# ScalarE and VectorE take the recorded order, and branch D's sums and attention's pauses move

## The chip, the cores and the metric

The kernel runs on one core of a Trainium2 chip. The metric is the device time of one execution in microseconds. Five engines of the core work beside each other: TensorE (PE in the profile, its weight loads PEld) multiplies matrices, ScalarE (ACT) applies functions element by element and copies, VectorE (DVE) does arithmetic on one or two tiles, GpSimd (POOL) does little here, and SyncE (SP) starts most DMAs. Each engine works through its own list of instructions in order, and semaphores make one engine wait for another.

## The reference

Two layers of a hybrid encoder over x (256 tokens, 2048 channels, float32), then a final RMSNorm:

```python
h = rms_norm(x, norm_g)
proj = h @ w_in                       # 2048 x 15104: inputs of the branches A, B, C, D, and four merge gates
ya = a_bg * depthwise_conv(a_cg * a_x, conv_a_w) * silu(a_z)                  # A: 3 taps
yb = gqa_attention(rope(rms_norm(q)), rope(rms_norm(k)), v) * silu(b_z)       # B: 8 query heads, 2 kv heads
yc = rwkv7_bidir(h, c_r, c_k, c_v, ...) * silu(c_z)                           # C: a recurrence in both directions
yd = silu(layer_norm(depthwise_conv(d_val * sigmoid(d_gate), dw_w))) * silu(d_z)   # D: 31 taps
bp = einsum('bskc,kcd->bskd', stack([ya, yb, yc, yd]), w_branch)              # four products 512 x 2048
x = x + (sum over branches of sigmoid(gates) * bp) @ w_out                    # 2048 x 2048
```

## The kernel before

**The stream of weights.** The weights of a layer come as 306 chunks of 128 x 1024 float32 (512 KB), 612 in all. SP starts a DMA for each into one of 4 buffers `raw` (`load`). ScalarE copies a chunk, rounded, to `hi` (`fetch`, 3 buffers), VectorE computes `lo` = raw - hi (`low`, 2 buffers). TensorE multiplies with both, the operand being held as a rounded part and a rest too. For most tiles (`tile_b`, two chunks, PSUM tile `mg`, 3 buffers) a chunk is 8 matmuls 512 wide on `hi`, then 8 matmuls 256 wide on `lo`, called the lo pass here. For a branch's product (`tile_branch`, PSUM tile `mb`) a chunk is 24 matmuls 256 wide. When chunk n begins on TensorE, `chunk` records `lo` of chunk n + 1 and `hi` of chunk n + 2; the two buffers of `lo` let lo n + 1 begin only when the lo pass of chunk n - 1 is over. After a `tile_b`, `whole` and `evac` move its sum out: a ScalarE copy of one half of PSUM, then a VectorE add of the other half, both short but on the same two engines. In the rows below, chunk 0 is the first of the kernel.

**The side work.** Everything else runs beside the stream: the norm at the layer's start (`normalise`), the head norms and rotary positions of attention (`head_rstd`, `norm_rope`), attention (`branch_b`), the convolutions (`branch_a`, `conv_d`, `branch_d`), the preparation of the recurrence for two pairs of heads and two directions (`rwkv`: decay, norm of k, cumulative products; `chunks`, and `inverses`, a triangular solve whose substitution is 31 pairs of dependent VectorE operations on 64 partitions), and the recurrence. These are Python generators. `pump`, called after each pair of matmuls while the program is recorded, advances a generator by its next piece when a planner's clocks allow it. A generator yields a pause: a positive number counts from now, a negative one (`HP` -2.5, `PM` -1.5, `LN` -3.6) from the time at which the planner expects the piece's last result. The planner charges each instruction a fixed price. The planner's clocks decide what is recorded between which matmuls.

**Who keeps that order.** `run` records both layers under `manual_schedule(engines={PE})`: TensorE's list is the recorded order. The lists of ScalarE and VectorE are laid out by the framework's scheduler, which moves `hi`, `lo`, evacuation copies and a few more (recorded under `high_priority`) ahead of side work and takes other instructions as it expects them to become ready.

**Reciprocal square roots.** `rsqrt` is, on ScalarE, a table load, a logarithm, another table load and an exponential. The norms of heads (`parts`, then `exact`) split a square into two rounded tiles `part`, of which one pair of buffers exists, and sum it with two matmuls into a PSUM tile `sd`.

Of the kernel before, what the change touches and what calls it, by code (L numbers as in the profile page):

```python
# [18 lines left out]
P = 128  # L19
# [6 lines left out]
CH = 64  # L26
# [185 lines left out]
class Kern:  # L212
# [26 lines left out]
    def __init__(self, ctx, tc, io):  # L239
        self.tc, self.io = tc, io  # L240
        self.now = self.due = self.landed = 0.0
        self.clk = {"vector": 0.0, "scalar": 0.0}
        self.ring = [0.0] * 4
        self.rushing = False
        self.next = dict(self.clk)
        self.nc = Clocked(self)
        pool = lambda name, space=None: ctx.enter_context(
            tc.tile_pool(name=name, bufs=1, space=space) if space else tc.tile_pool(name=name, bufs=1))
        self.cst = pool("cst")
        self.wp = pool("wp")  # L250
        self.sp = pool("sp")
        self.ps = pool("ps", PSUM)
        self.dr = pool("dr", DRAM)
        self.n = 0
        self.side = []
        self.cur = None
        self.arena = Arena(self.cst.tile([P, self.ARENA], F32, name="arena"), self.ARENA)
# [388 lines left out]
        yield 1.1  # L646


    def parts(self, x):

        self.n += 1
        n = int(np.prod(x.shape[1:]))
        t = self.wp.tile([P, 2, 512], F32R, tag="part", bufs=self.PARTS, name=f"part_{self.n}")
        hi, lo = t[:, 0, :n], t[:, 1, :n]
        view = lambda a: a.rearrange("p (a t) -> p a t", a=x.shape[1]) if len(x.shape) > 2 else a
        self.nc.scalar.activation(view(hi), x, AF.Copy)
        self.nc.vector.tensor_tensor(view(lo), x, view(hi).bitcast(F32), ALU.subtract)
        return hi, lo

    def exact(self, ps, stationary, parts):  # L660

        hi, lo = parts
        self.nc.tensor.matmul(ps, stationary, hi, start=True, stop=False)
        return self.nc.tensor.matmul(ps, stationary, lo, start=False, stop=True)

    def head_rstd(self, x):

        nc = self.nc
        out = self.a1()
        nc.scalar.activation(out, x, AF.Square)  # L670
        parts = self.parts(out)
        yield self.HP
        ps = self.pside()[:, :S]
        self.rsqrt(ps, 1.0 / 64, self.e_rms, out, self.exact(ps, self.bdr, parts))
        yield 0
        return out

    def norm_rope(self, x, rs, g, dst):
# [2 lines left out]
        nc.vector.scalar_tensor_tensor(xn, x, g, rs, ALU.mult, ALU.mult)  # L681
        t = self.a1()
        nc.vector.tensor_tensor(t, xn, self.cos, ALU.mult)
        parts = self.parts(xn)
        yield self.HP
        ps = self.pside()
# [86 lines left out]
    def branch_d(self, acc, convs, dz):  # L773
        nc = self.nc
        for i in range(NT):
            while len(convs) <= i:
                yield 0.5
            yield from convs[i]
        while self.merged < 1:
            yield 0.5  # L780
        ys = self.ys[3] = self.operand()
        yield 0
        sq = self.a([P, 2, S])
        nc.vector.tensor_tensor(sq[:, 0:2], acc[:, 0:2], acc[:, 2:4], ALU.add)
        nc.vector.tensor_tensor(sq[:, 0], sq[:, 0], sq[:, 1], ALU.add)
        yield self.LN
        ps = self.pside()
        nc.tensor.matmul(ps[:, :S], self.ones, sq[:, 0], start=True, stop=True)
        for i in range(NT):
# [8 lines left out]

        rs = self.a1()
        self.rsqrt(ps[:, :S], 0.25 / W, self.e_ln, rs, made)  # L800
        yield 0
        for i in range(NT):
            while len(dz) <= i:
# [16 lines left out]
    def rwkv(self, rkv, tl, cz):  # L820
# [5 lines left out]
        for d in range(2):  # L826
# [8 lines left out]
            for p0 in range(0, NT, 2):  # L835
                pp = slice(p0, p0 + 2)
                v5 = lambda x: x.rearrange("p a (c t) -> p a c t", c=NCH)
                while self.cv < p0 + 1:
                    yield 0.5
                yield from self.room(3136)  # L840
                lbs = []
                for i in range(2):
                    lb = self.a([P, 2, P])
                    nc.gpsimd.dma_start(lb[:LORA], self.io["lorab"][l, d, :, :, (p0 + i) * P:(p0 + i + 1) * P])
                    lbs.append(lb)
                yield 0.3
# [22 lines left out]
                for i in range(2):  # L869
                    p, lb = p0 + i, lbs[i]  # L870
                    ps = self.pside()
                    for j in range(2):
                        nc.tensor.matmul(ps[:, j * S:(j + 1) * S], lb[:LORA, j], tl[j][d][:LORA], start=True, stop=True)
                    self.f(lb)
                    nc.scalar.activation(flip(sg[:, i]), ps[:, :S], AF.Tanh, scale=0.5, bias=self.w0h[:, d * NT + p:d * NT + p + 1])
                    nc.scalar.activation(flip(ai[:, i]), ps[:, S:], AF.Tanh, scale=0.5, bias=self.a0h[:, d * NT + p:d * NT + p + 1])
                    yield 0.8
                parts = self.parts(rs)
                yield self.PM
                ps = self.pside()  # L880
# [6 lines left out]
                for i in range(2):  # L887
                    nc.vector.tensor_tensor_scan(sg[:, i], self.scan, sg[:, i], 0.0, ALU.mult, ALU.add)

                pi = self.a([P, 2, NCH, CH + 1])  # L890
                nc.vector.memset(pi[:, :, :, 0:1], 1.0)
                nc.scalar.activation(pi[:, :, :, 1:], v5(sg), AF.Exp, scale=-DECAY)
                pv = sg
# [23 lines left out]
                self.f(ai)  # L917
                yield 1.0
                nc.scalar.activation(dend[:, pp], pi[:, :, :, CH], AF.Copy)
                self.f(pi)  # L920
                yield 0
                parts = self.parts(r2)
                yield self.PM
                ps = self.pside()
# [25 lines left out]
            if d == 1:  # L950
                self.f(*rkv)
            self.cur.want = 0

            yield 4.0
            yield from self.room(2304)
# [31 lines left out]
            for p in range(NT):  # L987
# [68 lines left out]

                sq = self.a([P, 2, S])
                nc.scalar.activation(sq, y2, AF.Square)
                parts = self.parts(sq)
                yield self.PM  # L1060
                ps = self.pside()
# [70 lines left out]
    def chunks(self, n, out, bd, al, vv, kb, gs, rd):  # L1132
# [39 lines left out]
            if h == 0:  # L1172
                yield 0.6
        out.append((ex, mk, w))
        yield self.PM


    def layer(self, l):
# [28 lines left out]
            self.bdr, self.permr = rounded[:, 0], rounded[:, 1]  # L1207
        self.ys = [None] * 4
        self.merged = 0
        got = {}  # L1210
        gens = [[] for _ in range(4)]
        acc = [None] * 8
# [171 lines left out]
    def run(self):  # L1384
# [3 lines left out]
        self.consts()  # L1388
        self.first_x()

        with self.tc.manual_schedule(engines={mybir.EngineType.PE}):
            for l in range(DEPTH):
                self.layer(l)

# [124 lines left out]
```

## Time and profile before

| | |
|---|---|
| time, median of 3 runs | 1965.2 us (1964.5 to 1965.85) |
| the profiled execution: time, span | 1966.2 us, 1964.2 us |
| mean granted TensorE clock of the span | 0.994 |
| PE, DVE, ACT busy | 1921.9, 1444.4, 1262.0 us |
| `lo`: 612 on DVE | 748.5 us busy, 1.223 us each |
| `hi`: 612 on ACT | 646.8 us busy, 1.057 us each |
| ACT table loads | 62, 1.283 us each |

Busy time is the union of an engine's instructions. The span runs from the first to the last instruction that the profile counts; the execution's own time is 2.0 us longer. The first matmul starts at 9.4 us, since it waits for x.

### The profile page before, as it was taken

How to read it: one execution, taken by the hardware profiler on the slowest of the kernel's cores; microseconds unless marked ns; L12 is line 12 of the kernel's file. 1: busy time of each engine (PE TensorE's matmuls, PEld its weight loads, DVE VectorE, ACT ScalarE, POOL GpSimd, SP SyncE). 2: the span in 40 equal slices, each digit the busy share in tenths (PEclk: the TensorE clock that was granted, in tenths of full speed). 3: DMA queues.
4: the chain of work that ended last, by engine and by line, in shares of the span. 5: the costliest groups of instructions: out<-in, count | busy, mean ns of one | idle time of the engine just before them, and what ended most of it. 6: DMA issues, size and time to landing. Idle time of an engine off the chain costs nothing.

```text
span 1964.2 us, 32326 instructions
## 1 busy us (share of the span) xinstructions
PE 1921.9 (98%) x12190; PEld 1704.5 (87%) x12190; DVE 1444.4 (74%) x2500; ACT 1262.0 (64%) x2292; POOL 72.3 (4%) x117
## 2 busy tenths in 40 slices
PE   8999999999999999999999999999999999999997
PEld 6888788899988998998888887888989889989886
DVE  7867979977787556666687778799677875565665
ACT  7777577667647776554467766776666477765544
POOL 2001010000001000000000011000001010000000
PEclk9999999999999999999999999999999999999998
DMA  7555454455556445566655555444555564455653
GB/s 254 178 176 173 159 159 131 152 176 178 178 179 189 150 152 176 195 210 207 206 193 178 176 172 162 136 151 150 172 176 185 169 180 152 151 185 195 207 194 129
DMA packets 97692, 343.17 MB, mean 175 GB/s; under 512 B 11808, under 2 KB 12192, under 8 KB 97536
## 3 DMA queue, kind: packets, MB, share of 16 engines
q1 hardware_dynamic: 93312, 331.48, 51.2%
q0 software_dynamic: 3648, 8.59, 1.8%
q8 instruction: 95, 1.56, 0.3%
q10 hardware_dynamic: 576, 1.05, 0.1%
q14 instruction: 61, 0.50, 0.1%
HBM read 332.48 MB, written 8.39 MB: 174 GB/s over the span
## 4 chain that ended last, share of the span: by engine, by line
PE 95%; DVE 2%; ACT 1%; issue 0%; DMA 0%; DVEq 0%; SPq 0%; ACTq 0%
PE mg L201 76%; PE mb L201 10%; PE sd L201 10%; DVE arena L201 1%; DVE lo L201 1%; ACT bdE L201 1%; DMA arena<-xT 0%; ACT hi L201 0%; DVE slab L201 0%; ACT L175 0%; DVE part L201 0%; ACT bdS L201 0%; DVEq L1514 0%; ACT arena L201 0%; ACT slab L201 0%
## 5 line engine op out<-in xcount | busy, mean ns | idle before, releaser
L201 PE MATMUL mg<-slab,hi 128*128 128x512 f32 x4368 | 1141.6, 398 | 12.6 <-DVE slab L201 12.6
L201 DVE TENSOR_TENSOR lo<-raw,hi 128x1024 fp32r<-128x1024 f32 x612 | 748.5, 1223 | 355.7 <-PE mg L201 271.6
L201 ACT ACTIVATE hi<-raw 128x1024 fp32r<-128x1024 f32 x612 | 646.8, 1057 | 446.4 <-PE mg L201 286.1
L201 PEld LDWEIGHTS mg<-slab,hi 128*128 128x128 f32 x4368 | 780.4, 189 | 154.8 <-DVE slab L201 15.4
L201 PEld LDWEIGHTS mg<-slab,lo 128*128 128x128 f32 x4368 | 603.8, 191 | 45.0 <-issue 3.2
L201 PE MATMUL mg<-slab,lo 128*128 128x256 f32 x4368 | 636.7, 286 | 0.0
L201 DVE TENSOR_TENSOR arena<-arena 128x256 f32<-128x256 f32 (+17 forms) x394 | 166.1, 430 | 9.6 <-ACT arena L201 3.5
L201 DVE SCALAR_TENSOR_TENSOR arena<-arena,par 128x256 f32<-128x256 f32 x346 | 155.0, 481 | 5.1 <-ACT arena L201 3.5
L201 PE MATMUL mb<-slab,hi 128*128 128x256 f32 (+1 forms) x1040 | 154.3, 288 | 0.0
L201 PEld LDWEIGHTS mb<-slab,hi 128*128 128x128 f32 x1040 | 138.5, 194 | 1.1
L201 DVE TENSOR_TENSOR arena<-mg,arena 128x256 f32<-128x256 f32 x305 | 127.7, 419 | 13.6 <-ACT arena L201 7.3
L201 ACT ACTIVATE arena<-arena,b_gate 128x256 f32<-128x256 f32 x128 | 64.7, 505 | 72.8 <-DVE arena L201 72.6
L201 ACT ACTIVATE arena<-arena 128x256 f32<-128x256 f32 (+4 forms) x194 | 92.7, 497 | 25.7 <-DVE arena L201 23.8
L201 ACT ACTIVATE arena<-mg 128x256 f32<-128x256 f32 x241 | 89.4, 372 | 5.9 <-DVE arena L201 3.1
L175 ACT ACT_TABLE_LOAD x62 | 79.5, 1283 | 14.7 <-PE sd L201 12.5
L201 PE MATMUL mb<-slab,lo 128*128 128x256 f32 x528 | 87.0, 285 | 0.0
L201 DVE SCALAR_TENSOR_TENSOR arena<-arena,mb 128x512 f32<-128x512 f32 x64 | 43.9, 686 | 54.0 <-PE mb L201 51.5
L201 PEld LDWEIGHTS mb<-slab,lo 128*128 128x128 f32 x528 | 73.7, 192 | 0.4
L201 ACT ACTIVATE bdE<-sd 64x128 f32<-64x128 f32 x256 | 63.1, 269 | 9.0 <-PE sd L201 6.8
L201 ACT ACTIVATE arena<-sd 128x64 f32<-128x64 f32 (+4 forms) x122 | 40.4, 333 | 28.8 <-PE sd L201 26.7
L201 ACT ACTIVATE arena<-arena,par 128x256 f32<-128x256 f32 x88 | 43.0, 508 | 4.6 <-DVE arena L201 3.1
L201 PE MATMUL sd<-arena 96*128 96x256 f32 (+3 forms) x224 | 43.7, 338 | 0.0
(96 smaller groups left out, 1022.1 us busy)
## 6 DMA issues: line engine op xcount, KB each, us to landing
raw<-w SPq DMA_DIRECT2D x612, 512.0 KB, 3.4
arena<-xT SPq DMA_DIRECT2D x4, 512.0 KB, 8.4
scratch<-slab POOLq DMA_DIRECT2D x16, 128.0 KB, 3.0
scratch<-arena POOLq DMA_DIRECT2D x8, 256.0 KB, 4.1
arena<-xT SPq DMA_DIRECT2D x8, 256.0 KB, 3.7
x<-arena SPq DMA_DIRECT2D x8, 256.0 KB, 3.9
arena<-x SPq DMA_DIRECT2D x8, 256.0 KB, 3.8
arena<-lorab POOLq DMA_DIRECT2D x16, 96.0 KB, 3.1
```

The lines of the kernel that those rows point to most:

```text
L175: return f(out)
L201: return f(out, *args, **kw)
```

## The change

`manual_schedule` now covers TensorE, ScalarE and VectorE, so all three lists are the recorded order; priorities no longer move anything on them. Since a fixed order must not let two generators hold the one pair of `part` buffers crosswise, a flag `held` (`alone`) makes a generator wait, while the program is recorded, until the pair is free. The pause of `head_rstd` before its sums is doubled, the last pause of `chunks` goes from `PM` to `HP`. Branch D's sums, which were recorded once the first branch was merged, are recorded in a `lull` after the preparation of the recurrence's second direction, with a doubled pause; the result's slab is taken later. In `rwkv` two small tiles share one buffer.

```diff
+    def alone(self):
+        while self.held:
+            yield 0.2
+        self.held = True
...
     def exact(self, ps, stationary, parts):
         hi, lo = parts
+        self.held = False
...
         nc.scalar.activation(out, x, AF.Square)
+        yield from self.alone()
         parts = self.parts(out)
-        yield self.HP
+        yield 2 * self.HP
...
-        while self.merged < 1:
+
+        while not self.lull:
             yield 0.5
-        ys = self.ys[3] = self.operand()
-        yield 0
+        yield from self.room(800)
         sq = self.a([P, 2, S])
...
-        yield self.LN
+        yield 2 * self.LN
         ps = self.pside()
         nc.tensor.matmul(ps[:, :S], self.ones, sq[:, 0], start=True, stop=True)
...
         self.rsqrt(ps[:, :S], 0.25 / W, self.e_ln, rs, made)
+        while self.merged < 1:
+            yield 0.5
+        ys = self.ys[3] = self.operand()
+        self.cur.want = 0
...
             if d == 1:
                 self.f(*rkv)
             self.cur.want = 0
+            self.lull = d == 1
...
         out.append((ex, mk, w))
-        yield self.PM
+        yield self.HP
...
-        with self.tc.manual_schedule(engines={mybir.EngineType.PE}):
+        with self.tc.manual_schedule(engines={mybir.EngineType.PE, ACT, DVE}):
```

Three places show what this does to the lists. In the rows, `hi_..`, `lo_..` and `raw_..` are buffers of one chunk, `mg_..` is the PSUM tile that an evacuation reads, `arena` is the side work's memory, and the numbers in names are serial.

**The start.** ScalarE before, from the third `hi` on (`hi_13` is chunk 2's, `hi_22` chunk 3's, `hi_26` chunk 4's, `hi_29` chunk 5's; `rounded` is a constant that a DMA brings, `sd_14` the sum of squares of the first norm):

```order
9 L201 ACTIVATE hi_13_169<-raw_7_122 128x1024
10 L201 ACTIVATE arena_69<-arena_69 128x1024
11 L201 ACTIVATE arena_69<-mg_20_209 128x256
12 L201 ACTIVATE hi_22_228<-raw_8_125 128x1024
13 L201 ACTIVATE arena_69<-arena_69 128x1024
14 L201 ACTIVATE hi_26_256<-raw_21_226 128x1024
15 L201 ACTIVATE hi_29_278<-raw_25_254 128x1024
```

and of the change, from the same `hi` on:

```order
9 L201 ACTIVATE hi_13_169<-raw_7_122 128x1024
10 L201 ACTIVATE arena_69<-arena_69 128x1024 x3
11 L201 ACTIVATE rounded_203<-arena_69 128x256
12 L201 ACTIVATE hi_22_228<-raw_8_125 128x1024
13 L201 ACTIVATE arena_69<-mg_20_209 128x256
14 L201 ACTIVATE arena_69<-sd_14_179,eps_73 128x256
15 L175 ACT_TABLE_LOAD
16 L201 ACTIVATE arena_69<-arena_69 128x256
17 L201 ACTIVATE arena_69<-arena_69 96x256
18 L201 ACTIVATE hi_26_256<-raw_21_226 128x1024
```

The squares, `rounded` and the whole first norm have moved ahead of the `hi` of chunks 3 and 4. On SP the DMA that `rounded` waits for has moved ahead by four chunks, to right behind the DMA of chunk 6 (`raw_28`); on TensorE the matmul on `sd_14` has moved from the lo pass of chunk 7 to between chunks 2 and 3.

**A norm of k in the preparation of the recurrence** (the first of four in a layer, chunks 22 to 26). ScalarE before, `hi_106` being chunk 25's and `mg_100` the tile of chunks 22 and 23:

```order
74 L201 ACTIVATE hi_111_857<-raw_105_822 128x1024
75 L201 ACTIVATE bdR0_91<-rd_105 64x2x64 x2
76 L201 ACTIVATE bdR1_93<-rd_105 64x2x64 x2
77 L201 ACTIVATE arena_69<-mg_100_796 128x256
78 L175 ACT_TABLE_LOAD
79 L201 ACTIVATE arena_69<-arena_69 128x512
80 L175 ACT_TABLE_LOAD
81 L201 ACTIVATE arena_69<-arena_69,par0_71 128x256
82 L201 ACTIVATE hi_114_885<-raw_110_855 128x1024
83 L201 ACTIVATE arena_69<-arena_69 128x512
```

and of the change:

```order
64 L201 ACTIVATE hi_106_824<-raw_101_797 128x1024
65 L175 ACT_TABLE_LOAD
66 L201 ACTIVATE arena_69<-arena_69 128x512
67 L175 ACT_TABLE_LOAD
68 L201 ACTIVATE arena_69<-arena_69 128x512
69 L201 ACTIVATE arena_69<-mg_100_796 128x256
70 L201 ACTIVATE hi_111_857<-raw_105_822 128x1024
```

VectorE of the change at the same place (`sd_108` holds the norm's sums, `lo_112` is chunk 25's):

```order
79 L201 TENSOR_TENSOR lo_107_826<-raw_95_762,hi_102_799 128x1024
80 L201 TENSOR_SCALAR arena_69<-sd_108_839 128x512
81 L201 TENSOR_TENSOR arena_69<-mg_100_796,arena_69 128x256
82 L201 TENSOR_TENSOR lo_112_859<-raw_101_797,hi_106_824 128x1024
83 L201 TENSOR_SCALAR arena_69<-arena_69 128x512
```

The evacuation copy, which stood ahead of the first table load, now stands behind the whole root; the add that completes it stands ahead of chunk 25's `lo`, where before that `lo` stood first.

**The substitution of `inverses`** (chunks 62 to 72). VectorE before, from chunk 66's `lo` on:

```order
260 L201 TENSOR_TENSOR lo_289_2138<-raw_280_2074,hi_285_2110 128x1024
261 L201 TENSOR_TENSOR arena_69<-arena_69 64x231
262 L201 MEMSET arena_69 128x1
263 L201 TENSOR_TENSOR arena_69<-arena_69 64x21x11
264 L201 TENSOR_TENSOR arena_69<-arena_69 64x240
265 L201 TENSOR_TENSOR arena_69<-arena_69 64x20x12
266 L201 TENSOR_TENSOR arena_69<-arena_69 64x247
267 L201 TENSOR_TENSOR lo_295_2184<-raw_284_2108,hi_288_2136 128x1024
```

and of the change, between chunk 66's `lo`, which is the row ahead of these, and chunk 67's, which is the next:

```order
243 L201 TENSOR_TENSOR arena_69<-arena_69 64x207
244 L201 TENSOR_TENSOR arena_69<-arena_69 64x23x9
245 L201 TENSOR_REDUCE arena_69<-sd_289_2128 128x2
246 L201 TENSOR_SCALAR arena_69<-arena_69 128x2
247 L201 TENSOR_TENSOR arena_69<-arena_69 64x220
248 L201 TENSOR_TENSOR arena_69<-arena_69 64x22x10
249 L201 RECIPROCAL arena_69<-arena_69 128x2
250 L201 TENSOR_TENSOR arena_69<-arena_69 64x231
251 L201 TENSOR_TENSOR arena_69<-arena_69 64x21x11
252 L201 MEMSET arena_69 128x1 x2
253 L201 TENSOR_TENSOR arena_69<-mg_282_2088,arena_69 128x256
254 L201 TENSOR_TENSOR arena_69<-arena_69 128x256
```

The steps keep their number, but at this chunk all that was recorded between two `lo` now stands between them on VectorE too, the tile's add included.

## Rows read from the trace of the kernel before

**Rows 1.** The page, busy time of the engines.

```profile
PE 1921.9 (98%) x12190; PEld 1704.5 (87%) x12190; DVE 1444.4 (74%) x2500; ACT 1262.0 (64%) x2292; POOL 72.3 (4%) x117
```

**Rows 2.** The page, chain that ended last, by engine.

```profile
PE 95%; DVE 2%; ACT 1%; issue 0%; DMA 0%; DVEq 0%; SPq 0%; ACTq 0%
```

**Rows 3.** Waits of PE: what waited, for whom: us in total, times, longest.

```profile
PE mg L201 <- DVE slab L201: 12.6, 5, 9.4
PE sd L201 <- DVE arena L201: 4.6, 5, 2.1
PE sd L201 <- ACT part L201: 4.5, 2, 2.6
PE sd L201 <- ACT bdS L201: 2.9, 2, 1.4
PE sd L201 <- ACT bdE L201: 2.8, 2, 1.4
PE sd L201 <- DVE part L201: 1.2, 3, 0.7
```

**Rows 4.** Windows: us; PE, PEld, DVE, ACT, POOL busy; PEclk, DMA share, GB/s.

```profile
223.90:226.40 2.50, 0.58 (x3) 0.15 (x2) 2.43 (x8) 0.83 (x2) 0.00 (x0) 1.00 0.52 164
226.40:229.90 3.50, 3.29 (x13) 2.84 (x14) 2.82 (x9) 2.73 (x4) 0.00 (x0) 0.51 0.09 35
...
1554.20:1557.70 3.50, 3.50 (x18) 3.42 (x17) 3.25 (x8) 1.13 (x3) 0.00 (x0) 0.51 0.02 5
```

**Rows 5.** Timeline of all engines at chunks 23 to 25: start, us, engine, what.

```profile
82.18 0.63 PE L201 MATMUL sd<-part,rounded 128*128 128x512 f32 x2
...
82.84 0.69 DVE L201 TENSOR_SCALAR arena<-sd 128x512 f32<-128x512 f32 x1 [0.18 <-PE sd L201]
...
83.24 2.00 PE L201 MATMUL mg<-slab,hi 128*128 128x512 f32 x8
...
84.28 0.39 ACT L201 ACTIVATE arena<-mg 128x256 f32<-128x256 f32 x1
84.68 1.28 ACT L175 ACT_TABLE_LOAD   x1
84.70 0.42 DVE L201 TENSOR_TENSOR arena<-mg,arena 128x256 f32<-128x256 f32 x1
...
85.97 0.63 ACT L201 ACTIVATE arena<-arena 128x512 f32<-128x512 f32 x1
86.03 2.00 PE L201 MATMUL mg<-slab,hi 128*128 128x512 f32 x8
...
87.87 1.11 PE L201 MATMUL mg<-slab,lo 128*128 128x256 f32 x8
```

**Rows 6.** Timeline of DVE at chunk 23: two scans.

```profile
79.29 1.26 DVE L201 TENSOR_TENSOR_SCAN arena<-consts,arena 128x256 f32<-128x256 f32 x2
```

**Rows 7.** Timeline at the substitution, chunks 63 to 72: lo, lo passes, four steps.

```profile
203.10 1.23 DVE L201 TENSOR_TENSOR lo<-raw,hi 128x1024 fp32r<-128x1024 f32 x1
...
208.34 1.11 PE L201 MATMUL mg<-slab,lo 128*128 128x256 f32 x8
...
213.84 1.71 DVE L201 TENSOR_TENSOR arena<-arena 64x231 f32<-64x231 f32 x4
...
240.06 1.11 PE L201 MATMUL mg<-slab,lo 128*128 128x256 f32 x8
```

**Rows 8.** Timeline of the start: chunk 2's lo, chunk 3, the constant's DMA and use.

```profile
17.73 1.23 DVE L201 TENSOR_TENSOR lo<-raw,hi 128x1024 fp32r<-128x1024 f32 x1 [0.70 <-ACT hi L201]
...
21.18 2.00 PE L201 MATMUL mg<-slab,hi 128*128 128x512 f32 x8
...
28.88 0.91 SPq L201 DMA_DIRECT2D arena<-cst  x1
...
33.21 0.42 ACT L201 ACTIVATE rounded<-arena 128x256 fp32r<-128x256 f32 x1 [0.48 <-DMA arena<-cst]
```

**Rows 9.** Timeline at the boundary of the layers: TensorE waits.

```profile
985.47 0.50 PE L201 MATMUL mg<-slab,hi 128*128 128x512 f32 x1 [1.45 <-DVE slab L201]
```

More of the change, by code (lines that the diff above doesn't have):

```diff
@@ L243, in __init__ @@
         self.ring = [0.0] * 4
-        self.rushing = False
+        self.rushing = self.held = False
         self.next = dict(self.clk)
@@ L683, in norm_rope @@
         nc.vector.tensor_tensor(t, xn, self.cos, ALU.mult)
+        yield from self.alone()
         parts = self.parts(xn)
@@ L840, in rwkv @@
                 yield from self.room(3136)
+                buf = self.a([P, 2 * NCH * (CH + 1)])
                 lbs = []
                 for i in range(2):
-                    lb = self.a([P, 2, P])
+                    lb = buf[:, i * 2 * P:(i + 1) * 2 * P].rearrange("p (j n) -> p j n", j=2)
                     nc.gpsimd.dma_start(lb[:LORA], self.io["lorab"][l, d, :, :, (p0 + i) * P:(p0 + i + 1) * P])
@@ L873, in rwkv @@
                         nc.tensor.matmul(ps[:, j * S:(j + 1) * S], lb[:LORA, j], tl[j][d][:LORA], start=True, stop=True)
-                    self.f(lb)
                     nc.scalar.activation(flip(sg[:, i]), ps[:, :S], AF.Tanh, scale=0.5, bias=self.w0h[:, d * NT + p:d * NT + p + 1])
@@ L877, in rwkv @@
                     yield 0.8
+                yield from self.alone()
                 parts = self.parts(rs)
@@ L888, in rwkv @@
                     nc.vector.tensor_tensor_scan(sg[:, i], self.scan, sg[:, i], 0.0, ALU.mult, ALU.add)
-                pi = self.a([P, 2, NCH, CH + 1])
+                pi = buf.rearrange("p (a c t) -> p a c t", a=2, c=NCH)
                 nc.vector.memset(pi[:, :, :, 0:1], 1.0)
@@ L919, in rwkv @@
                 nc.scalar.activation(dend[:, pp], pi[:, :, :, CH], AF.Copy)
-                self.f(pi)
+                self.f(buf)
                 yield 0
+                yield from self.alone()
                 parts = self.parts(r2)
@@ L1058, in rwkv @@
                 nc.scalar.activation(sq, y2, AF.Square)
+                yield from self.alone()
                 parts = self.parts(sq)
@@ L1209, in layer @@
         self.merged = 0
+        self.lull = False
         got = {}
```

## The prediction

> **What bounds the kernel now.** The page's busy times come first: TensorE works in 98% of the span, VectorE in 74%, ScalarE in 64% [rows 1]. The chain that ended last says the same of the end: 95% of it is TensorE [rows 2]. So the time is TensorE's own work plus its waits, and a change that gives TensorE the same matmuls, as this one does, can act only on the waits and on the clock. PE's waits are the view that matters then: 28.6 us in the six groups of the table, 9.4 of it the start's wait for x, which the change leaves alone; 19.2 us are left, none longer than 2.6 us [rows 3]. The windows show what stands behind a long one. In 223.9 to 226.4 TensorE is busy 0.58 of 2.50 us, and in the 3.5 us behind it the granted clock is 0.51, the lower of its two levels (1.2 GHz); the same 0.51 stands at 1554.2 [rows 4]. There are four such stretches, each right behind a wait of over 2 us, two of them for `part` and two for branch D's sums; I found none behind shorter waits. One costs 3.5 x 0.49 = 1.7 us, four 6.8 us. All that is to be had is thus 19.2 + 6.8 = 26.0 us, 1.3% of the time.
>
> The second question is how much slack ScalarE and VectorE have. A chunk is 2.79 us on TensorE (83.24 to 86.03) and its lo pass stands 1.84 us behind its start (86.03 to 87.87) [rows 5]. Chunk 25's `lo` can begin 0.2 us after chunk 24 starts, when its buffer comes free, and is done 1.23 us later, at 84.67: 3.2 us ahead of its pass. That is the margin in the steady stretches, and no `lo` can be made earlier, since there are two buffers. What delays a `lo` by more than 3.2 us stops TensorE. Before, the scheduler puts each `lo` ahead of the side work that waits; the change puts it behind all that was recorded ahead of it.
>
> **What the change takes away.** The longer pauses and the earlier sums of D act on the four waits of over 2 us, the recorded order on the small ones, whose short chains no longer stand behind whatever the scheduler found ready. The boundary of the layers keeps its wait of 1.45 us [rows 9], since its chain is the same; I take 24 of the 26 us as gone, and 20 as the low end.
>
> **What it adds.** Five places, priced from the order and the rows.
>
> *The start.* Chunk 2's `lo` ends at 18.96 and frees the buffer for chunk 6's DMA, behind which the constant's DMA now stands. From the issue of that DMA to the start of `rounded` it took 4.3 us (28.88 to 33.21) [rows 8], so `rounded` runs from 23.3 to 23.7, and chunk 3's `hi`, now behind it, is done 1.06 us later at 24.8. Chunk 3 started at 21.18 [rows 8]: 3.6 us lost. Then a copy (0.39), the logarithm, a table load (1.28), the exponential and a tanh (0.4 each, for their 256 columns, an estimate between the 0.39 of the copy and the 0.63 of 512 columns [rows 5]) and the next `hi` take 3.9 to 4.0 us where TensorE needs 2.8: 1.2 more. I take 5, between 3 (a faster DMA) and 6 (the matmul on the sums, which now stands ahead of chunk 3 too, comes late).
>
> *Eight norms of k.* In the rows of chunk 23 the sums end at 82.81. Their clamp takes 0.69 from 82.84 on, to 83.53; then a table load 1.28, the logarithm 0.63, a table load, the exponential (0.63, as the logarithm), the copy that now stands behind it 0.39, the add 0.42 and the `lo` behind that 1.23: 89.39, for a pass at 87.87 [rows 5]. So 1.5 us each, and before nothing, since the copy stood at 84.28, ahead of the table load. Four in a layer: 12 us. The low end is 0.2 each, if the first table load runs while its data are awaited; 12 is the high end too. Each of these roots has two table loads on that path, and the page of the Trainium skill "ScalarE: Activation LUTs", section "What ACT_TABLE_LOAD costs", gives 1283 ns for a load and about 1380 ns for a drain behind it. The trace agrees on the first and not on the second: the load at 84.68 takes 1.28 and the logarithm starts at 85.97 [rows 5]; with two drains a norm would cost 4.3 us instead of 1.5.
>
> *The norm of the second pair of heads* (chunks 45 to 55, once a layer, the first direction). There the recorded order has, between chunk 48's `lo` and chunk 49's, four two-input operations of 0.42, two scans (1.26 [rows 6]), and then an add whose copy on ScalarE stands behind two exponentials of the scans' result: 1.7 + 1.26 + 2 x 0.63 + 0.39 + 0.42 + 1.23 = 6.2 us. With the full margin ahead of it 2.79 + 3.2 = 6.0 us are to be had, and 0.2 is lost; with none, as behind the norm just priced, 3.4 are. I take 3.4, so 6.8 for two layers; the low end is 0.2 each, the high end 8 each, if the tiles behind it (chunks 51 and 55 have such adds) are late as well.
>
> *The substitution* (chunks 63 to 72). From the end of chunk 63's `lo` to the end of chunk 72's, VectorE's list now has 9 `lo` (11.0 us), 42 steps of the substitution, 17 other operations on 256 columns (7.1), and two reductions with small ones (1.9). Four steps take 1.71, so 0.43 each [rows 7]; I take 0.41, as the first are narrower: 17.2. That is 37.2 us. TensorE went from the one pass to the other in 31.7 us (208.34 to 240.06) [rows 7], of which 1.9 were the wait for `part` and 1.7 the low clock [rows 4]: 28.1 without them. VectorE needs 9.1 us more than TensorE, and chunk 63's `lo` was done 4.0 us ahead of its pass (204.33, 208.34) [rows 7], so 5.1 us are lost in each layer, whatever waits come on top. I take 10 for both; 7.6 with steps of 0.38, 22 if the tiles' adds, which stand in this list as well, wait about 3 us each for a copy behind a table load, twice a layer.
>
> *The rest.* At the boundary, seven small operations and six fills for the next layer stand ahead of a `lo`, and one ScalarE copy ahead of the other: 2 us at most; I take 2. In the recurrence and at branch D's sums, whose two adds stand ahead of a `lo` again, though three chunks ahead of their matmul, I choose 1 us each per layer, 4, with 0 and 8 as the ends: the list shows the same adds as before, at other chunks, and the trace doesn't price them.
>
> *The clock.* Three of these waits are over 2 us (the start, twice the second pair of heads): by rows 4 another 1.7 each, 5; the substitution may add some, so 10 at most, and nothing if the waits come in small pieces.
>
> **The sum.** 5 + 12 + 6.8 + 10 + 2 + 4 + 5 = 44.8 added, 24 taken away: 20.8. The profiled execution took 1966.2, 1.0 above the median: 1987.0, and against the median 1986. All low ends give 3 + 1.6 + 0.4 + 7.6 = 12.6 less 24, so 1954; all high ends 6 + 12 + 16 + 22 + 2 + 8 + 10 = 76 less 20, so 2021.
>
> **The rivals.** *Faster, about 1959.* The first table load of a root doesn't wait with its logarithm but is over when the clamp is. Its place is chunk 25's `lo` and the seven like it: a norm then costs 0.2 and not 1.5, chunk 48 finds its margin, and 10.4 + 6.4 us of the sum and 3.4 of the clock fall away. 24.6 are left against 24, so it decides with what *the rest* costs: if the two lists absorb the 6 us there, 18.6 are added, 1966.2 - 5.4 = 1960.8, or 1959.8 against the median, and 1958 if the start's DMA lands faster. For it speaks that ScalarE and VectorE have a third and a quarter of the time free [rows 1]; against it that the free time lies elsewhere than in chunks 63 to 72, and that before, at 84.68, the first load began only when the copy was over, at 84.67, so that the rows don't show a load ahead of its data [rows 5]. *No change.* The same, but the rest costs what I chose: 24.6 added, 1966. *Much slower, about 2007.* Every late `lo` is followed by the low clock, and the substitution's adds wait for ScalarE; the high ends of the substitution and of the heads alone give 12 + 9.2 more, 2007. *By the page's drain* the norms would take 8 x 2.8 = 22 us more, 2008 too; the row at 85.97 speaks against it.
>
> **How the numbers follow.** Slower as forecast or more: 0.70, of which 0.12 for 2007 and above (0.02 of it by the drain); faster: 0.22, as it needs the early load and most of the rest at nothing; no change, within 0.2% or 3.9 us, which is about what a measurement of this kernel can tell: 0.08. The range reaches from the sum of the low ends, 1953 against the median, and 2 us below it, as one of them may vanish, to between the much slower cases and the sum of the high ends: 1951 to 2014. The forecast's own range is 1972 to 2002.
>
> **What would show it.** Right: PE waiting for `lo` on VectorE as the largest group of waits, 3 to 4 us for `hi` at chunk 3, waits of about 1.5 us at chunk 25 with the copy behind the second exponential, VectorE without a pause from chunk 63 to 72, the waits for `part` and for branch D's sums gone. Wrong: waits for `lo` of under 20 us in all; a table load that runs ahead of the clamp; chunk 3 starting before 23 us; or `part` and the sums waited for as before. I would be wrong upward if the windows behind the new waits show a clock of 0.5 more than three or four times.

## The result, and the profile after

The changed kernel takes 2048.8 us (median of 4 runs, 2045.5 to 2049.05), against 1965.3 for the kernel before in the same job: 1.042 times as long (95% interval 1.040 to 1.044). The direction was forecast, the size, 83.5 us instead of 21, was not. The profiled execution took 2048.8 us, with a span of 2046.7.

The busy times of the page after, which answer to [rows 1]:

```profile
PE 1949.6 (95%) x12190; PEld 1707.2 (83%) x12190; DVE 1467.9 (72%) x2500; ACT 1254.6 (61%) x2292; POOL 71.5 (3%) x117
```

Each engine has as many instructions as before. PE's waits after, in the same form as [rows 3] (what waited, for whom: us, times, longest):

```profile
PE mg L201 <- DVE lo L201: 37.4, 37, 2.3
PE sd L201 <- DVE arena L201: 11.3, 9, 4.7
PE mg L201 <- DVE slab L201: 9.5, 1, 9.5
PE sd L201 <- ACT bdR L201: 8.6, 4, 2.6
PE sd L201 <- ACT arena L201: 6.5, 8, 2.0
PE mb L201 <- DVE lo L201: 4.5, 8, 0.9
PE mg L201 <- ACT hi L201: 1.8, 1, 1.8
```

The waits for `lo`, which before had no row, come to 41.9 us. But the groups on `sd`, the matmuls of the side work, have grown too: 26.4 us in three groups here, for results of ScalarE and VectorE that had 5.6 before; all waits on `sd` come to 30.0 us, against 17.0. `part` has left the table (0.5 us). With four small groups the waits are 73.7 us without the start's 9.5, against 20.2: 53.5 more. The mean granted clock is 0.989 instead of 0.994, which is 22.5 and 11.8 us of the spans, so 10.7 more. The remaining 18 of the 82.5 us are told in the last section.

### The profile page after: what moved, and what is told of

It reads as the page before. It is cut to its first block, busy times and chain, and to the rows that moved or that the text cites. A ratio compares the mean times of both kernels' runs of the same rounds, so it can differ in the third digit from the quotient of the medians.

```text
span 2046.7 us, 32156 instructions
## 1 busy us (share of the span) xinstructions
PE 1949.6 (95%) x12190; PEld 1707.2 (83%) x12190; DVE 1467.9 (72%) x2500; ACT 1254.6 (61%) x2292; POOL 71.5 (3%) x117
## 3 DMA queue, kind: packets, MB, share of 16 engines
q10 hardware_dynamic: 576, 1.05, 0.1%
## 5 line engine op out<-in xcount | busy, mean ns | idle before, releaser
L201 DVE TENSOR_TENSOR lo<-raw,hi 128x1024 fp32r<-128x1024 f32 x612 | 743.0, 1219 | 75.9 <-ACT hi L201 29.4
L201 ACT ACTIVATE hi<-raw 128x1024 fp32r<-128x1024 f32 x612 | 631.8, 1049 | 55.8 <-PE mg L201 28.8
L201 DVE TENSOR_TENSOR arena<-arena 128x512 f32<-128x512 f32 (+18 forms) x394 | 170.1, 434 | 35.9 <-ACT arena L201 26.2
L201 DVE SCALAR_TENSOR_TENSOR arena<-arena,par 128x256 f32<-128x256 f32 x346 | 162.6, 481 | 12.1 <-ACT arena L201 7.0
L201 ACT ACTIVATE slab<-arena 128x512 fp32r<-128x512 f32 (+1 forms) x64 | 33.5, 523 | 86.3 <-DVE arena L201 86.3
L201 ACT ACTIVATE arena<-sd,arena 128x128 f32<-128x128 f32 (+1 forms) x80 | 32.3, 406 | 64.7 <-DVE arena L201 35.1
L201 DVE SCALAR_TENSOR_TENSOR arena<-arena,mb 128x512 f32<-128x512 f32 x64 | 43.8, 684 | 28.1 <-PE mb L201 27.8
L201 DVE SCALAR_TENSOR_TENSOR slab<-arena,slab 128x512 fp32r<-128x512 f32 (+1 forms) x64 | 35.7, 557 | 30.1 <-ACT slab L201 30.1
```

The lines of the kernel that those rows point to most:

```text
L201: return f(out, *args, **kw)
```

## The experiments

All comparisons below are with the kernel before in the same job, at 1964.8 to 1965.7 us. Four kernels first separate the recorded order from the moved parts, and the two engines.

**The change without the recorded order of ScalarE and VectorE.**

```diff
-        with self.tc.manual_schedule(engines={mybir.EngineType.PE, ACT, DVE}):
+        with self.tc.manual_schedule(engines={mybir.EngineType.PE}):
```

> The kernel after with only TensorE's list in recorded order; the pauses, the flag and branch D's earlier sums stay. My theory (the recorded lists of ScalarE and VectorE cost it all): between 1945 and 1970 us, with the waits for part and for D's sums shorter than before and waits of TensorE for lo near 0. Rival (the moved pauses and sums, which give TensorE another list, cost a good part): 1990 us or more.

Measured: 1959.6 us, ratio 0.9965 (0.9952 to 0.9978), faster than before by 6. PE's waits:

```profile
PE mg L201 <- DVE slab L201: 12.1, 6, 8.7
PE sd L201 <- ACT part L201: 4.6, 2, 2.3
PE sd L201 <- DVE part L201: 2.2, 4, 0.7
...
PE mb L201 <- DVE lo L201: 0.5, 1, 0.5
```

So the order alone costs 89 us. TensorE's list is the same in this kernel and in the change but for the matmul on the first sums, so it serves below as the base: stretches of chunks can be compared one by one. The waits for `part`, which the doubled pause was to shorten, are still there (4.6 and 2.2 us); what has gone are the waits for branch D's sums.

**The kernel before with all three lists recorded** (the same line, the other way round, in the kernel before).

> The kernel before, all three lists in recorded order, without the flag, the longer pauses and D's earlier sums. My theory: as slow as the kernel after or slower, 2045 to 2075 us, since the waits for part and D's sums come on top. Rival (the moved pauses and sums cost a good part of the 83 us): 2020 or less.

Measured: 2044.9 us, 1.0404 (1.0388 to 1.0419). My theory's side in the cause: the order costs 79 us without any moved part (the time is 0.1 us under the range that I gave).

**One engine's order at a time** (`{PE, DVE}` and `{PE, ACT}` in that line).

> The kernel after with the lists of TensorE and VectorE in recorded order, ScalarE's laid out by the scheduler. If VectorE's list is the main cost (lo stands behind all that was recorded ahead of it): 2020 to 2050 us. If ScalarE's list is (copies and hi behind roots): 1960 to 1985. If the two only cost together: both this and the next below 1990.

> The kernel after with the lists of TensorE and ScalarE in recorded order, VectorE's laid out by the scheduler. If VectorE's list is the main cost: 1965 to 1990 us, the start's loss of about 5 us for hi among it. If ScalarE's is: 2020 to 2050.

Measured: 2063.0 us (1.0502, 1.0485 to 1.052) and 2027.1 us (1.0312, 1.0296 to 1.0327). The second fits the case of ScalarE's list, the first is beyond that of VectorE's, and I had put them as opposites: each engine's order costs much by itself, VectorE's alone even more than both, and with ScalarE's alone `lo` is hardly waited for (0.3 us), yet 67 us are lost.

**The start.** Only TensorE's list recorded over the first six tiles.

```diff
+            if l == 0 and n == 6:
+                self.ctx.__exit__(None, None, None)
+                self.ctx = self.tc.manual_schedule(engines={mybir.EngineType.PE, ACT, DVE})
+                self.ctx.__enter__()
...
```

> The kernel after with only TensorE's list recorded over the first 12 chunks, all three from there on. My theory (the start's loss is the squares, the rounded constant and the first root standing ahead of the hi of chunks 3 and 4, and is not caught up later): chunks 2 to 5 take 8.4 us instead of 18.5, the time 2037 to 2042. Rival (what is lost at the start gives later waits their margin back): 2044 or more.

Measured: 2038.1 us (1.0368, 1.0352 to 1.0383). From chunk 2's start to chunk 5's it takes 8.4 us instead of 18.5; chunks 5 to 22 take 0.4 more, later stretches 0.7 more. My theory's side in the time, but the loss is twice what the prediction had for it. The timeline of the change there:

```profile
21.31 1.23 DVE L201 TENSOR_TENSOR arena<-arena 128x1024 f32<-128x1024 f32 x1 [1.12 <-ACT arena L201]
22.57 1.06 ACT L201 ACTIVATE arena<-arena 128x1024 f32<-128x1024 f32 x1 [1.29 <-DVE arena L201]
...
25.64 0.33 SPq L201 DMA_DIRECT2D arena<-cst  x1
...
26.12 1.22 PE L201 MATMUL sd<-arena,consts 128*128 128x256 f32 x2 [4.70 <-DVE arena L201]
27.77 0.42 ACT L201 ACTIVATE rounded<-arena 128x256 fp32r<-128x256 f32 x1 [4.14 <-DMA arena<-cst]
28.09 1.04 ACT L201 ACTIVATE hi<-raw 128x1024 fp32r<-128x1024 f32 x1
...
29.18 3.62 PE L201 MATMUL mg<-slab,hi 128*128 128x512 f32 x8 [1.84 <-ACT hi L201]
```

ScalarE's squares and VectorE's adds wait for each other by turns, since the next square goes into the buffer of the last one: I had the constant's DMA as the late one, but the sums, whose matmul now stands ahead of chunk 3, come at 26.1 first, and the constant at 27.8 (its DMA was issued at 25.6, not right behind 18.96: SP first waits 6.2 us for a VectorE instruction on `arena`). During the wait of 4.7 us the granted clock falls to 0.50, the lower level, until 32.5, and the 8 wide matmuls at 29.18 take 3.62 us, where before they took 2.00 [rows 8]:

```profile
25.64:32.47 6.83, 4.51 (x10) 2.99 (x10) 1.79 (x4) 4.18 (x8) 1.67 (x3) 0.50 0.17 48
```

(A window, with the columns of [rows 4].)

**The first pair's norm of k recorded behind the evacuation** instead of ahead of it (`copies` counts the evacuations in `whole`).

```diff
...
                 yield self.PM
+                seen = getattr(self, "copies", 0)
+                while p0 == 0 and self.copies == seen:
+                    yield 0.1
                 ps = self.pside()
                 self.exact(ps, self.bdr, parts)
```

> The kernel after, in which the norm of k of the first pair of heads is recorded behind the next evacuation instead of ahead of it. If the root ahead of the copy makes the 2.6 and 3.3 us that chunks 22 to 32 and 328 to 338 lose: both fall under 0.5, and the second direction's norm of that pair gives 0.5 to 1 each, 2040 to 2044 us in all. If VectorE's list is late there for another reason: both stretches stay above 2 us.

Measured: 2074.1 us (1.0557, 1.0541 to 1.0573). Chunks 22 to 32 and 328 to 338 lose 1.1 us each instead of 2.6 and 3.3, so the place is the norm's, though more is left than I expected. The whole is 25 us slower than the change: the merges (chunks 183 to 282 and 489 to 588) take 32 us more. That what was recorded later moves all the side work behind it is my reading of it, not shown. A local gain says nothing on the total here.

The norm itself went as forecast, in the timeline of the change at chunk 25:

```profile
91.84 0.69 DVE L201 TENSOR_SCALAR arena<-sd 128x512 f32<-128x512 f32 x1 [1.10 <-PE sd L201]
...
92.56 1.28 ACT L175 ACT_TABLE_LOAD   x1 [2.73 <-DVE arena L201]
...
94.50 1.28 ACT L175 ACT_TABLE_LOAD   x1
...
95.80 0.63 ACT L201 ACTIVATE arena<-arena 128x512 f32<-128x512 f32 x1
96.34 0.37 ACT L201 ACTIVATE arena<-mg 128x256 f32<-128x256 f32 x1
...
97.08 1.22 DVE L201 TENSOR_TENSOR lo<-raw,hi 128x1024 fp32r<-128x1024 f32 x1
...
98.35 1.22 PE L201 MATMUL mg<-slab,lo 128*128 128x256 f32 x8 [1.32 <-DVE lo L201]
```

The table load waits with its data (2.73 us for the clamp), so the faster rival's condition doesn't hold; the exponential starts at 95.80, 1.30 us after the second load began, right behind the load's own 1.28. The drain of about 1380 ns behind a load, which the Trainium skill's page "ScalarE: Activation LUTs", section "What ACT_TABLE_LOAD costs", gives, is thus not seen here either.

**A third buffer for lo.**

```diff
-    FAR = 1
+    FAR = 0
...
-            w[1] = self.wtile("lo", 2, F32R)
+            w[1] = self.wtile("lo", 3, F32R)
...
-        if self.ready:
-            self.low(self.ready[0])
+        for r in self.ready[:2]:
+            self.low(r)
```

> The kernel after with a third buffer for lo, made one chunk earlier in the recorded order, and one buffer less for raw. My theory (ScalarE's and VectorE's lists lag behind in bursts longer than the 3.2 us by which lo is early; 2.8 us more cover most of them): TensorE's waits for lo fall from 41.9 us to under 15, the time to 2005 to 2020 us. Rival (the lists lack throughput over long stretches, so that more margin only puts the same wait off): waits for lo above 28 us, time above 2030.

Measured: 2210.3 us (1.1246, 1.1229 to 1.1263), a miss for both: TensorE's waits for `lo` fall to 1.9 us, as my theory had it, but the time is far above its range, since TensorE now waits 84.8 us for `hi` and 90.9 for the operands of its matmuls on `sd`. From the tables of VectorE's and ScalarE's waits:

```profile
DVE lo L201 <- ACT hi L201: 476.2, 367, 4.9
...
ACT arena L201 <- DVE arena L201: 440.3, 257, 6.9
...
ACT hi L201 <- DMA raw<-w: 63.4, 42, 4.1
```

Recorded right behind its `hi`, `lo` now makes VectorE's whole list wait for ScalarE, 476 us in all, where the change has 29.4. That idle time isn't all lost, but it swamped the margin; and the buffer that `raw` gave up shows in the last line (18.4 us in the change). What a longer margin alone would bring stays open.

**The substitution's steps further apart** (`XSTEP` 1.5 instead of 1.0).

> The kernel after with 1.5 us instead of 1.0 between the steps of the substitution. If the substitution's rows between two lo are what VectorE falls behind on in chunks 58 to 102 and 165 to 183: those stretches, 22.6 and 7.5 us per layer longer than with TensorE's list alone recorded, lose a third to a half of that, the time 2020 to 2035. If it costs in chunks 62 to 73 alone: 2037 to 2042. If not the steps but the roots and copies among them cost there: 2046 or more.

Measured: 2086.3 us (1.0615, 1.0597 to 1.0633). The stretches named do lose less: chunks 62 to 73 3.5 us instead of 6.3, and 165 to 183 0.2 on average instead of 7.5. But the total is worse: the substitution's steps are recorded over more chunks, what comes behind it moves towards the merges, and there chunks 183 to 282 and 489 to 588 take 45 us more than in the change.

**The last pause of chunks** back at `PM`, in the change and in the kernel with TensorE's list alone.

> The kernel after with the last pause of chunks back at the short one. If that pause makes the 7 us per layer of chunks 80 to 102, which the kernel before with all lists recorded has only 1.4 of: 2034 to 2040 us. Rival (the loss there comes with the doubled pause of the head norms or with the flag): 2046 to 2051.

> The kernel with only TensorE's list recorded and all else of the change, but the last pause of chunks back at the short one. If the longer pause is worth something: 1961 to 1965 us; if the 6 us that the moved parts bring are branch D's sums and the head norms alone: 1957 to 1961.

Measured: 2050.4 us (1.0433, 1.0418 to 1.0449) and 1958.5 us (0.9965, 0.9952 to 0.9978): the pause does nothing in either that these runs could tell.

**Only side work bound.** In the base, every ScalarE and VectorE instruction of side work is put behind the one recorded before it on its engine, by an order that needs no semaphore; `hi`, `lo` and the evacuation's copy and add are left to the scheduler. Without these the two lists are those of the change, but for seven pairs of neighbours on VectorE that change places.

```diff
+    def chain(self, name, i):
+        if self.chained and not self.stream_op and name in ("vector", "scalar"):
+            prev = self.tail.get(name)
+            if prev is not None:
+                self.tc.add_manual_dep(i.ins, prev.ins.name,
+                                       mybir.DependencyInfo(mybir.DependencyClass.NoSync, mybir.DependencyReason.DATA),
+                                       reason="recorded order")
+            self.tail[name] = i
+        return i
```

> The kernel after in which the recorded order binds only the side work of ScalarE and VectorE (each such instruction stands behind the one recorded before it on its engine); hi, lo and the evacuations are placed by the scheduler with their priority. The side work's order on both engines is that of the kernel after, row by row. My theory (the loss is hi, lo and the evacuations standing behind side work that waits or is late): TensorE waits for lo under 5 us, 1955 to 1985 us in all. Rival (pieces of side work stand behind one another, and TensorE's other matmuls, recorded early, wait for them): 2000 us or more, with waits of the matmuls on sd for ScalarE and VectorE at 40 us or more.

Measured: 2029.5 us (1.034, 1.032 to 1.036): the rival's side. PE no longer waits for `lo` at all, and yet the kernel is 70 us above the base, against 89 with everything bound:

```profile
PE sd L201 <- ACT bdR L201: 22.5, 6, 9.5
PE sd L201 <- ACT part L201: 19.4, 8, 4.4
PE mg L201 <- DVE slab L201: 13.6, 5, 9.7
PE sd L201 <- DVE part L201: 7.0, 11, 1.4
PE sd L201 <- DVE arena L201: 5.2, 4, 2.4
```

These are not the waits of the change with those for `lo` taken away. All waits on `sd` come to 66.0 us here, to 30.0 in the change and to 10.0 in the base; `part` has 26.4 here and 0.5 in the change. So side work held in order is enough for 70 us, but the 89 of the change are not to be split into 70 and 19: in the change TensorE waits 43.7 us for `lo` and `hi`, and less for the rest. That the one wait lets the operands of the other catch up fits this, and isn't shown.

**The evacuations bound too**, only `hi` and `lo` free.

> As the run before, but the evacuations keep their recorded place among the side work; only hi and lo are free. If lo standing in VectorE's list is the loss by itself: within 10 us of the run before. If the copies behind roots and the adds behind them are a large part (an add that comes late holds the side work behind it, and the PSUM tile): 15 to 40 us above it.

Measured: 2080.6 us (1.0585, 1.0568 to 1.0602), 51 above the run before, beyond both cases. That an evacuation which keeps its place holds the side work behind it until its tile is done, or stands behind side work itself, fits this, but is argued. Why it comes out above the change, where `lo` and `hi` are bound too, stays open. What goes with it is on record: TensorE's waits without the start's are 92.6 us, against 73.7 in the change, and the mean granted clock is 0.973, against 0.989.

**One engine's side work bound**, and **the substitution free**:

```diff
-        if self.chained and not self.stream_op and name in ("vector", "scalar"):
+        if self.chained and not self.stream_op and name == "vector":
```

(`"scalar"` in the other), and, in `rwkv`, with both:

```diff
                 tm = self.a([P, n, m])
+                self.stream_op = True
...
+                self.stream_op = False
                 self.f(tm)
```

> As ch_free, with the recorded order binding VectorE's side work alone. If the loss is VectorE's order: 2015 to 2035 us. If the loss needs both orders (a ScalarE piece held behind one that waits for VectorE): below 1995.

> As ch_free, with the recorded order binding ScalarE's side work alone. If the loss is VectorE's order: 1960 to 1980 us. If ScalarE's order holds side work up as well: 1995 or more.

> As ch_free, with the 31 pairs of the substitution also free of the recorded order on VectorE. If the 70 us that ch_free still loses are side work held behind the substitution (62 pairs of 0.4 us in each direction, which the planner charges less for): 1965 to 1985 us, chunks 62 to 102 and 165 to 183 within 3 us of the kernel with TensorE's list alone recorded. Rival (any two pieces of side work hold each other up the same way): 2005 us or more.

Measured: 2000.4 us (1.0178, 1.0161 to 1.0195) with VectorE's, between its two cases, 2003.5 us (1.0194, 1.0179 to 1.021) with ScalarE's, where ScalarE's order holds work up as well, and 2017.8 us (1.0264, 1.0249 to 1.028) with both but the substitution, the rival's side. So the substitution explains 12 of the 70 us, not all; and each engine's order costs some 40 us, more together than when both are bound (70). That one wait then covers the other is likely, but the table shows more than that: what VectorE's order alone loses from chunk 183 on, 14.1 us, isn't lost when both are bound.

What each stretch takes beyond the base, both layers added, from the starts of the chunks' first matmuls (profiled executions; the base's span is 1953.8 us, and 1955.7 its time, the shortest of its five executions, so that the change stands 92.9 above it here):

| chunks of a layer | change | side work bound | VectorE's | ScalarE's |
|---|---|---|---|---|
| 2 to 22, first layer | 8.9 | 0.5 | 0.5 | -0.8 |
| 22 to 44: first norms of k | 6.5 | 0.4 | 0.5 | 0.9 |
| 44 to 58: second pair | 19.6 | 9.0 | 5.5 | 4.2 |
| 58 to 80: substitution, attention | 22.3 | 18.3 | 16.8 | 6.8 |
| 80 to 125: recurrence, first direction | 14.0 | 14.6 | 1.9 | 18.4 |
| 125 to 165: second preparation, merges | 7.2 | 6.7 | 6.3 | 1.0 |
| 165 to 183: second substitution ends | 15.0 | 22.8 | -0.5 | 18.0 |
| 183 on | -2.2 | -2.3 | 14.1 | -2.3 |
| boundary | 1.2 | 0.4 | 0.2 | 0.4 |
| sum | 92.5 | 70.4 | 45.3 | 46.6 |

The largest single wait of the kernel with ScalarE's side work bound shows how side work holds TensorE up. Timeline at chunk 181 of that kernel:

```profile
608.18 3.42 DVE L201 TENSOR_TENSOR arena<-arena 64x192 f32<-64x192 f32 x10
...
611.97 0.42 ACT L201 ACTIVATE arena<-arena 128x256 f32<-128x256 f32 x1 [0.55 <-DVE arena L201]
...
614.14 0.60 ACT L201 ACTIVATE arena<-arena,par 128x256 f32<-128x256 f32 x1 [1.76 <-DVE arena L201]
614.77 0.42 ACT L201 ACTIVATE arena<-arena 128x256 f32<-128x256 f32 x1
615.10 0.61 ACT L201 ACTIVATE bdM<-slab 64x128 f32<-64x128 f32 x2
...
615.72 0.63 ACT L201 ACTIVATE bdR<-rd 64x128 f32<-64x128 f32 x2
...
616.40 1.22 PE L201 MATMUL sd<-bdR,slab 128*128 128x128 f32 x4 [7.50 <-ACT bdR L201]
```

The copies `bdM` and `bdR` read tiles of the preparation and wait for nothing themselves. They stand behind two tanh and an affine of branch D's, which wait for VectorE, which is at the substitution. TensorE's matmul on `bdR` was recorded where the planner thought them done, and waits 7.5 us. In the change the same rows are at 641 to 643.7:

```profile
641.40 0.60 ACT L201 ACTIVATE arena<-arena,par 128x256 f32<-128x256 f32 x1 [1.45 <-DVE arena L201]
...
642.36 0.61 ACT L201 ACTIVATE bdM<-slab 64x128 f32<-64x128 f32 x2
642.98 0.63 ACT L201 ACTIVATE bdR<-rd 64x128 f32<-64x128 f32 x2
...
643.66 1.22 PE L201 MATMUL sd<-bdR,slab 128*128 128x128 f32 x4 [2.61 <-ACT bdR L201]
```

**The doubled pause of the head norms taken back** in the base.

> The kernel with TensorE's list alone recorded and all else of the change, but the pause of the head norms back at the single one. If branch D's earlier sums bring the 6 us by themselves: 1957 to 1961 us, with the waits for part at 4.6 us or more. If the doubled pause brings half of it or more: 1962.5 to 1966, with longer waits for part in chunks 62 to 73.

Measured: 1975.4 us (1.0056, 1.0039 to 1.0072), outside both cases. The waits for `part` don't grow (4.5 us), but TensorE waits 5.4 us at once for an `arena` tile of ScalarE and 4.5 for one of VectorE, and chunks 183 to 232 and 489 to 538 take 7.7 and 6.7 us longer than before. The 6 us belong to the moved parts as a set; which of them brings what stays open.

## Why the prediction was wrong

**What bounds the kernel** was right: TensorE's waits and its clock, with what a wait costs beyond its row (the last section). So was the direction, and that the two lists held in order are the cause: 2048.8 against 1959.6 us with the moved parts, and 2044.9 against 1965.7 without them, show it from both sides.

**The sum by kind of loss** shows which steps failed (us, change against before, profiled executions):

| | forecast | measured |
|---|---|---|
| waits for `lo` and `hi` | 39.8 | 43.7 |
| TensorE's other waits | -17.2 | 9.8 |
| low clock | -1.8 | 10.7 |
| in none of these | 0 | 18.3 |
| sum | 20.8 | 82.5 |

(Forecast: 44.8 added, of which 5 for the clock; 24 taken away, of which 6.8 for the clock.) So late `lo` are the largest group of waits, as the prediction said, and nearly of the size that it gave them, though by luck in part: the start has less of them than forecast and the other places more. What it had wrong is the other three rows.

**What the change takes away: 24 us** is the first step that failed. The waits of [rows 3] for `part`, `bdE`, `bdS` and the boundary's slab (which was to keep its wait) have indeed shrunk to a few us in the change. But a recorded order makes other waits of the same kind: I took "short chains no longer stand behind whatever the scheduler found ready" for a gain, and the matmuls on `sd` wait 30.0 us in the change instead of 17.0. Nor do the moved parts bring 24 us by themselves: with the scheduler's order they give 6.

**The start: 5** was 8.9 with the low clock (chunks 2 to 22; chunks 2 to 5 alone lose 10.1), for which I had added 1.7 to it. The place held; the step that failed is the date of the sums and of the constant's DMA, as the squares and adds take turns: 4.7 us of wait for the sums and then 1.8 for `hi`, where I had 3.6 for `hi` alone.

**Eight norms of k: 12, and the second pair: 6.8.** The first chain was right to 0.1 us: 1.6 us more at chunk 25, by the rows that the prediction named. Stretches 22 to 58 and 125 to 165 lose 33.3 us, of which 18.8 and 3.4 of the clock were forecast. The waits for `lo` there are 19.8 us and the low clock 5.1; most of the excess is in none of the rows above. The second pair alone loses 9.9 and 9.7 per layer, near the high end of 8 beside its norm.

**The substitution: 5 a layer.** Chunks 62 to 73 lose 6.3 and 6.4. The size was near, but by luck: from the end of chunk 63's `lo` to that of chunk 72's it took 37.5 us, where I had 37.2 of work without a pause. VectorE is busy only 32.5 us of them, 15.1 with the steps for which I had 17.2, and waits 3.7 us for ScalarE in between:

```profile
243.50:245.90 2.40, 0.62 (x3) 0.19 (x1) 1.97 (x4) 2.40 (x5) 0.00 (x0) 1.00 0.01 3
247.50:250.90 3.40, 3.40 (x12) 2.71 (x11) 3.23 (x8) 0.45 (x2) 0.00 (x0) 0.50 0.69 260
228.61:266.13 37.52, 33.08 (x172) 26.16 (x171) 32.52 (x77) 16.63 (x33) 0.00 (x0) 0.95 0.38 131
```

(windows of the change, columns as in [rows 4]; the first holds a wait of 1.84 us for `lo`, the second the low clock behind it.) With `hi`, `lo` and evacuations free those chunks lose 2 us a layer, so the excess of work that I added up there is mostly absorbed when `lo` may pass.

**The rest: 4, and the boundary: 2.** The boundary measured 1.2. The rest is the added term that failed most. I chose 1 us for the recurrence and D's sums per layer, on the ground that the list shows the same adds as before. Chunks 80 to 125 and 165 to 183 lose 29 us. Of TensorE's waits there 14.3 us are for operands of its matmuls on `sd` and 4.4 for `lo`: at the largest of the 14.3, the rows at 641 to 643.7, ScalarE's copies for the recurrence stand behind branch D's pieces, which wait for VectorE. Every price of mine asked when a `lo` or `hi` is late; none asked the same of the operands of TensorE's other matmuls, which are fixed in its list as well. In the change these are 30.0 of the 73.7 us of waits; the run with only side work bound shows that such waits alone can cost 70 us.

**The clock: 5** stood for three stretches of low clock. The change has nine beside the one at the end that both kernels have: eight of 3.4 us and the start's 6.8, together 17.1 us, so my own sign of being wrong upward came true. The four old ones (6.8) are gone, which leaves the 10.7 of the means. Three of the nine:

```profile
169.00:172.40 3.40, 3.30 (x12) 3.01 (x13) 3.29 (x8) 0.66 (x1) 0.00 (x0) 0.50 0.50 154
643.45:646.85 3.40, 3.19 (x15) 3.19 (x16) 2.33 (x7) 1.75 (x4) 1.39 (x3) 0.50 0.89 243
1295.40:1298.80 3.40, 3.40 (x11) 2.16 (x11) 3.14 (x7) 1.18 (x2) 2.58 (x5) 0.50 0.78 188
```

They stand behind waits of 2.29 us for `lo`, 2.61 for `bdR` and 1.78 for `bdR`. "Over 2 us", as the prediction had it of the four before, was a misreading: the wait for `part` ahead of 226.4 is 1.92 us, 2.50 less 0.58 [rows 4].

**The rivals.** The faster one needed a table load ahead of its data; the row at 92.56 excludes it. The much slower one named the clock behind late `lo` and the substitution's adds waiting for ScalarE, 2007; both are there in part, but the time went beyond it, and beyond the sum of all high ends, 2021, for what no rival had: the waits on `sd` and the cost beyond the wait rows.

## What to carry to other kernels

When a kernel fixes the order of an engine that a scheduler has arranged, price not only the stream that must not stop but each instruction that another engine's fixed list waits for: whatever stands ahead of it in the queue, and what that waits for in turn. Here a planner whose clocks are good enough to place matmuls was not good enough to give the order of all queues: it charges (0.06 + 231/960) x 1.05 = 0.32 us for a step of 64x231 that takes 0.43 [rows 7], and where something falls behind its clocks, the scheduler lets ready work pass and a recorded order doesn't (that the prices are the cause is argued, not shown). Leaving the weight stream free is not enough either, as the 70 us with only side work bound show. The version to keep is the change without the two recorded lists, 1959.6 us; with the short pause it is 1958.5, which these runs can't tell from it.

## What the runs showed of the hardware that I had not expected

A wait of TensorE costs more than its row says. At chunk 25 the row gives 1.32 us, but the chunk takes 4.38 us instead of 2.79, 0.27 more. The weight loads of before and of the change at the lo pass (the matmuls behind them start at 87.87 and at 98.35):

```profile
87.64 1.13 PEld L201 LDWEIGHTS mg<-slab,lo 128*128 128x128 f32 x8
```

```profile
98.35 1.02 PEld L201 LDWEIGHTS mg<-slab,lo 128*128 128x128 f32 x8 [1.74 <-DVE lo L201]
```

Before, the first load begins 0.23 us ahead of its matmul, under the matmuls of the chunk's first half; in the change only when the wait is over, so it is idle for 1.74 us and not 1.32. Chunk by chunk against the base, the 53 chunks of the change that have one wait, at full clock, and none in the base, take 0.27 us more than the base's chunk and the wait together (median; 0.18 to 0.49), 14.8 us in all. That is most of the 18 of the 82.5 us that are neither in the wait rows nor in the clock. That the late weight load is the reason fits the rows, but no run changes it by itself.
